# A four-layer latent-diffusion trunk in fp32: boundary and SiLU operations in place in PSUM, and the root of a row sum in six pointer steps

## The chip, the cores and the metric

The kernel runs on one core of a Trainium2 chip. The metric is the device time of one execution in microseconds (us); the kernel before took 2905.99 us, the median of three runs (2902.37 to 2906.01). The engines are TensorE (PE; PEld is its weight load), VectorE (DVE), ScalarE (ACT), GpSimd (POOL) and SyncE (SP, which issues the DMAs). Each works through its own queue in order; semaphores make one wait for another. SBUF is the working memory of 128 partitions; PSUM is the smaller memory into which PE writes, here eight banks of 128 x 512 fp32.

## What is computed

A trunk of four layers over 256 context tokens and 256 latent tokens of width 1024. Layers 0 and 3 mix tokens by differential attention, layer 1 by windowed grouped-query attention, layer 2 by a bidirectional Mamba-2 scan. Each mixer is followed by a SwiGLU feed-forward network (FFN). Every sub-layer is wrapped like this, with shift, scale and gate from a conditioning vector (adaLN); the last layer handles the latent tokens only:

```python
def rmsnorm(t, g):
    tf = tf * lax.rsqrt(jnp.mean(tf * tf, axis=-1, keepdims=True) + NORM_EPS)
...
    h_lat = h_lat + m_lat[:, 2] * rmsnorm(o_lat, norm_g[i, 1])
    u_lat = modulate(rmsnorm(h_lat, norm_g[i, 2]), m_lat[:, 3], m_lat[:, 4])
    h_lat = h_lat + m_lat[:, 5] * rmsnorm(swiglu(u_lat, ffn_w_in[i], ffn_w_out[i]), norm_g[i, 3])
```

So between any two blocks of matmuls each token row needs a root of the mean square of the sub-layer's output, a residual add, a root of the mean square of the sum, a scaling, and the adaLN modulation.

## The kernel before

**Tiling.** The 512 tokens are four tiles of 128: 0 and 1 are the context (stream `c`), 2 and 3 the latents (stream `l`). `hall` holds the residual stream h with tokens on the partitions, `uhall` and `ulall` the modulated input u with features on the partitions, split into a high part (rounded for the fast fp32 matmul) and the low remainder. Every product is three matmuls per 128-deep slice: high by high, low by high, high by low (`lin`, L285 to L287; `lin_tokens`, L295 to L297). Weights stream in by DMA; for each block ACT makes the high part (L261) and POOL subtracts it from the raw block, `wl = wr - wh`, 128 x 1024 (L263).

**A boundary.** The out-projection of a mixer, and of an FFN, ends in `project`: for each tile and half x of the 1024 features a PSUM bank `mm` is filled (L507); an FFN adds the partial sum in `o` (L511); `gated` takes the squares with their row sum on ACT (L429, junk output to tag `tm`) and multiplies by the gate row on DVE (L430). After the second half `residual` computes the root (L436 and `rsqrt`) and adds to h in one operation over 1024 features (L439). `after` then runs `prenorm`: squares of h (L447), root (L448 and `rsqrt`), scaling of one half by ACT (L456) and one by DVE (L454), eight transposes on PE into two `sm` banks (L460), modulation into a tile of tag `tm` alternately by ACT (L475) and DVE (L473), the high part by ACT (L477) and the low part by DVE (L478). The FFN's `unit` fills a bank `mm` and a bank `sc` (L555, L556), takes SiLU on ACT (L560), the product on DVE into the SBUF tile `hd` (L561), and splits it (L563, L564).

**Order and buffers.** A scheduler fixes the order on each engine before the program runs, from estimates of its own. The transposes of L460 thus stand at fixed places between the matmuls of other tiles. PSUM's eight banks are divided: `mm` three, `sc` two, `sm` two, `ad` one (which the scheduler also uses for other tiles at times). Tag `tm` has two buffers in SBUF. The adaLN vectors are finished by `ada_flush` (L346 is one of its DVE lines).

Of the kernel before, what the change touches and what calls it, by code (L numbers as in the profile page):

```python
# [22 lines left out]
NTT = NT // P  # L23
DEPTH = 4
# [153 lines left out]
class Trunk:  # L178
# [206 lines left out]

    def stat(self, groups, div):
# [38 lines left out]
    def gated(self, src, t, x, row, ss):  # L425

        nc = self.nc
        q = self.t([P, 512], "tm", 2)
        nc.scalar.activation(q, src, AF.Square, scale=1.0 / 32, accum_out=ss[:, x : x + 1])  # L429
        nc.vector.tensor_tensor(out=self.om[t][:, 512 * x : 512 * x + 512], in0=src, in1=row, op=AL.mult)  # L430

    def residual(self, t, ss):

        nc = self.nc
        y, m = (self.t([P, 1], f"rs_{x}1", 4) for x in ("y", "m"))
        nc.vector.tensor_scalar(out=m, in0=ss[:, 0:1], scalar1=ss[:, 1:2], scalar2=EPS, op0=AL.add, op1=AL.add)  # L436
        self.rsqrt(y, m, 1)
        h = self.hall[:, t, :]
        nc.vector.scalar_tensor_tensor(out=h, in0=self.om[t], scalar=y, in1=h, op0=AL.mult, op1=AL.add)  # L439

    def normed(self, t):

        nc = self.nc
        y, m, ss = (self.t([P, 1], f"rs_{x}1", 4) for x in ("y", "m", "s"))
        n = self.t([P, D], "sq", 2)
        h = self.hall[:, t, :]
        nc.scalar.activation(n, h, AF.Square, scale=1.0 / 32, accum_out=ss)  # L447
        nc.vector.tensor_scalar(out=m, in0=ss, scalar1=EPS, scalar2=None, op0=AL.add)  # L448
        self.rsqrt(y, m, 1)
        out = []  # L450
        for g in range(2):
            r = slice(512 * g, 512 * g + 512)
            if g:
                nc.vector.tensor_scalar(out=n[:, r], in0=h[:, r], scalar1=y, scalar2=None, op0=AL.mult)  # L454
            else:
                nc.scalar.activation(n[:, r], h[:, r], AF.Copy, scale=y)  # L456
            ps = self.psum("sm")
            for k in range(4):
                c = 512 * g + k * P
                nc.tensor.transpose(ps[:, k * P : (k + 1) * P], n[:, c : c + P], self.cst["ident"])  # L460
            out.append(ps.rearrange("p (k t) -> p k t", k=4))
        return out

    def modulate(self, src, shift, scale, t, g):
# [15 lines left out]
    def prenorm(self, shift, scale, t):  # L480
        for g, ps in enumerate(self.normed(t)):
            self.modulate(ps, shift, scale, t, g)
# [12 lines left out]
    def project(self, blocks, ah, al, streams, rows, after, add):  # L495
# [3 lines left out]
        for s in streams:  # L499
            ts = TILES[s]  # L500
            ss = {t: self.t([P, 2], "ss", 4) for t in ts}
            halves = [(t, x) for t in ts for x in range(2)]
            if s == streams[0]:
                halves = [(t, x) for x in range(2) for t in ts]
            for t, x in halves:
                ps = self.psum("mm")
                self.lin_tokens(ps, blocks[x], ah, al, t)  # L507
                src = ps
                if add:
                    src = self.om[t][:, 512 * x : 512 * x + 512]  # L510
                    nc.vector.tensor_tensor(out=src, in0=ps, in1=src, op=AL.add)  # L511
                self.gated(src, t, x, rows[s, x], ss[t])
                if x:
                    self.residual(t, ss[t])
                    after(t)
# [29 lines left out]
    def ffn(self, i, u, streams, pool, gate, after):  # L545
# [5 lines left out]
        def unit(j, wg, wu, s):  # L551
# [6 lines left out]
            hd = self.t([P, NT], "hd", 2, pool=pool)  # L558
# [879 lines left out]
```

## Time and profile before

| what | value |
|---|---|
| median of three runs | 2905.99 us |
| the profiled execution | 2899.41 us, span 2897.6 us |
| mean granted clock of TensorE | 0.961 |
| PE busy | 2620.8 us (90%) |
| DVE, ACT, POOL busy | 1574.4, 1236.4, 1098.3 us |
| POOL's weight subtractions, L263 | 356 of 2432 ns and 49 of 2426 ns |
| DMA | 355.40 MB, mean 123 GB/s |

A busy share says how much of the span an engine worked, not which engine held the others up: that is read from the list of waits, from the timeline of a stretch, and from the idle time that stands in brackets before an instruction, with the instruction that released it. The granted clock is the share of TensorE's full clock in a stretch.

### The profile page before, as it was taken

What the parts mean: (1) busy time and instruction counts of PE and PEld (TensorE: products, weight loads), DVE (VectorE), ACT (ScalarE), POOL (GpSimd) and SP (SyncE); (2) the same over time, 40 slices, a digit from 0 to 9 for tenths busy, and PEclk for the clock granted to TensorE, in tenths of its full rate; (3) what the DMA queues carried; (4) which work ended last, traced back from release to release, by engine and by line L of the source; (5) the groups of instructions that cost most, each with busy time, mean ns of one, the idle gap of its engine ahead of it and who ended that gap; (6) DMA issues with size and microseconds to landing.
All of it is one profiled execution on the core that took longest, in us unless ns stands there. A gap on an engine that the chain in (4) does not pass through costs nothing. (4 is left out here: it accounts for less than half of the span.)

```text
span 2897.6 us, 37494 instructions
## 1 busy us (share of the span) xinstructions
PE 2620.8 (90%) x14134; PEld 2110.0 (73%) x14134; DVE 1574.4 (54%) x2955; ACT 1236.4 (43%) x2439; POOL 1098.3 (38%) x525
## 2 busy tenths in 40 slices
PE   6999989999889989999888888879899998897898
PEld 3777677777776787777686666667777776786797
DVE  4676652222577662222588898866522226667444
ACT  4555443222357643222345555554432224554543
POOL 2322044334321053333333444433343343334585
PEclk8999999999999999999998999999999999999899
DMA  7433335544221145544231111132344442323352
GB/s 290 138 109 121 131 128 184 173 173 150 88 94 45 44 138 175 175 174 149 82 97 37 59 44 62 63 105 96 121 176 175 174 145 86 101 86 126 124 182 88
DMA packets 108325, 355.40 MB, mean 123 GB/s; under 512 B 14064, under 2 KB 24688, under 8 KB 105840
## 3 DMA queue, kind: packets, MB, share of 16 engines
q1 hardware_dynamic: 107568, 351.66, 36.0%
q8 instruction: 111, 1.82, 0.3%
q10 hardware_dynamic: 576, 1.34, 0.1%
q14 instruction: 70, 0.57, 0.1%
HBM read 329.36 MB, written 13.63 MB: 118 GB/s over the span
## 5 line engine op out<-in xcount | busy, mean ns | idle before, releaser
L263 POOL TENSOR_TENSOR wl<-wr,wh 128x1024 fp32r<-128x1024 f32 x356 | 863.5, 2432 | 1499.3 <-ACT wh L261 1360.0
L261 ACT ACTIVATE wh<-wr 128x1024 fp32r<-128x1024 f32 x356 | 376.0, 1057 | 809.4 <-PE mm L286 291.8
L285 PE MATMUL mm<-uh,wh 128*128 128x512 f32 (+1 forms) x1496 | 529.9, 355 | 16.3 <-ACT uh L477 15.0
L286 PE MATMUL mm<-ul,wh 128*128 128x512 f32 (+1 forms) x1496 | 526.9, 352 | 0.1
L287 PE MATMUL mm<-uh,wl 128*128 128x512 f32 (+1 forms) x1496 | 526.7, 352 | 0.0
L561 DVE TENSOR_TENSOR hd<-sc,sg 128x512 f32<-128x512 f32 (+1 forms) x100 | 56.9, 568 | 603.6 <-PE sc L287 599.0
L285 PEld LDWEIGHTS mm<-uh,wh 128*128 128x128 f32 x1496 | 289.3, 194 | 73.7 <-ACT uh L477 15.9
L287 PEld LDWEIGHTS mm<-uh,wl 128*128 128x128 f32 x1496 | 289.4, 193 | 34.4 <-issue 3.6
L286 PEld LDWEIGHTS mm<-ul,wh 128*128 128x128 f32 x1496 | 289.8, 194 | 32.5 <-issue 1.5
L285 PE MATMUL sc<-uh,wh 128*128 128x512 f32 (+1 forms) x800 | 273.7, 342 | 0.0
L287 PE MATMUL sc<-uh,wl 128*128 128x512 f32 (+1 forms) x800 | 273.7, 342 | 0.0
L286 PE MATMUL sc<-ul,wh 128*128 128x512 f32 (+1 forms) x800 | 273.6, 342 | 0.0
L296 PE MATMUL mm<-wh,hid 128*128 128x512 f32 x616 | 244.6, 397 | 0.0
L297 PE MATMUL mm<-wl,hid 128*128 128x512 f32 x616 | 244.0, 396 | 0.0
L295 PE MATMUL mm<-wh,hid 128*128 128x512 f32 x616 | 243.6, 396 | 0.0
L564 DVE TENSOR_TENSOR hid<-hd,hid 128x512 fp32r<-128x512 f32 (+1 forms) x100 | 207.5, 2075 | 65.8 <-ACT hid L563 65.8
L285 PEld LDWEIGHTS sc<-uh,wh 128*128 128x128 f32 x800 | 153.1, 191 | 17.6 <-issue 0.8
L286 PEld LDWEIGHTS sc<-ul,wh 128*128 128x128 f32 x800 | 153.2, 191 | 16.9
L287 PEld LDWEIGHTS sc<-uh,wl 128*128 128x128 f32 x800 | 153.2, 192 | 16.8
L595 DVE TENSOR_TENSOR o<-mm,o 128x512 f32<-128x512 f32 x84 | 58.0, 691 | 157.8 <-PE mm L297 157.8
L295 PEld LDWEIGHTS mm<-wh,hid 128*128 128x128 f32 x616 | 115.7, 188 | 35.9 <-ACT hid L563 4.2
L263 POOL TENSOR_TENSOR wl<-wa,wh 128x1024 fp32r<-128x1024 f32 x49 | 118.9, 2426 | 59.2 <-ACT wh L261 58.8
(300 smaller groups left out, 4851.5 us busy)
## 6 DMA issues: line engine op xcount, KB each, us to landing
wa<-in_adaw SPq DMA_DIRECT2D x192, 512.0 KB, 5.2
wr<-in_fin SPq DMA_DIRECT2D x154, 512.0 KB, 3.5
wr<-in_fout SPq DMA_DIRECT2D x77, 512.0 KB, 3.5
wr<-in_ssi SPq DMA_DIRECT2D x40, 512.0 KB, 3.5
wr<-in_daqk SPq DMA_DIRECT2D x24, 512.0 KB, 3.8
wa<-in_fin SPq DMA_DIRECT2D x22, 512.0 KB, 3.6
hspill<-h SPq DMA_DIRECT2D x8, 1024.0 KB, 4.0
h<-hspill SPq DMA_DIRECT2D x8, 1024.0 KB, 6.3
```

What stands on the lines that cost most here:

```text
L261: nc.scalar.activation(h, raw, AF.Copy)
L263: eng.tensor_tensor(out=l, in0=raw, in1=f32(h), op=AL.subtract)
L285: mm(out, wh, ah[ka][:, a:b], start=j == 0, stop=False)
L286: mm(out, wh, al[ka][:, a:b], start=False, stop=False)
L287: mm(out, wl, ah[ka][:, a:b], start=False, stop=j == len(todo) - 1)
L295: mm(out, ah[ka][:, tk], wt.h[:, kw, :], start=j == 0, stop=False)
L296: mm(out, al[ka][:, tk], wt.h[:, kw, :], start=False, stop=False)
L297: mm(out, ah[ka][:, tk], wt.l[:, kw, :], start=False, stop=j == len(todo) - 1)
L561: nc.vector.tensor_tensor(out=hd[:, :w], in0=pu[:, :w], in1=sg[:, :w], op=AL.mult)
L564: nc.vector.tensor_tensor(out=hl[:, a:b], in0=hd[:, :w], in1=f32(hh[:, a:b]), op=AL.subtract)
L595: nc.vector.tensor_tensor(out=o, in0=ps, in1=o, op=AL.add)
```

## The change

In `project` the second half goes to a bank `sc` instead of `mm`; the added partial sum, the gate product and the second half of the residual are written back into the bank they were read from. `residual` is two operations of 512 features, the first into `hall`, the second into PSUM, and a new ACT copy, `settle`, brings the latter to `hall` behind the transposes. The squares of h are taken in two halves. `modulate` writes back into the transposes' bank, and the FFN's product back into its `sc` bank. `rsqrt1` replaces `rsqrt` for one column: six operations of one form (TENSOR_SCALAR, whose scalars may be pointers to a value per partition) in place of nine of three forms; `rsqrt` stays for the rows of several columns in `stat`.

```diff
+G = 1024.0 / 27
...
+    def rsqrt1(self, m):
+        ts = self.nc.vector.tensor_scalar
+        y, b, a = (self.t([P, 1], f"rs_{x}1", 4) for x in "yba")
+        ts(out=b.bitcast(I32), in0=m.bitcast(I32), scalar1=-0.5, scalar2=1597463007.0 - 2.0**31, op0=AL.mult, op1=AL.add)
+        ts(out=a, in0=b, scalar1=b, scalar2=m, op0=AL.mult, op1=AL.mult)
+        ts(out=a, in0=a, scalar1=-10.0 / 3, scalar2=a, op0=AL.add, op1=AL.mult)
+        ts(out=b, in0=a, scalar1=5.0, scalar2=b, op0=AL.add, op1=AL.mult)
+        ts(out=a, in0=b, scalar1=b, scalar2=m, op0=AL.mult, op1=AL.mult)
+        ts(out=y, in0=a, scalar1=-64.0 / 3, scalar2=b, op0=AL.add, op1=AL.mult)
+        return y
...
-    def gated(self, src, t, x, row, ss):
...
+    def squares(self, src, ss):
         q = self.t([P, 512], "tm", 2)
-        nc.scalar.activation(q, src, AF.Square, scale=1.0 / 32, accum_out=ss[:, x : x + 1])
-        nc.vector.tensor_tensor(out=self.om[t][:, 512 * x : 512 * x + 512], in0=src, in1=row, op=AL.mult)
+        self.nc.scalar.activation(q, src, AF.Square, scale=G / 32, accum_out=ss)
...
+    def root(self, ss):
+        m = self.t([P, 1], "rs_m1", 4)
+        self.nc.vector.tensor_scalar(
+            out=m, in0=ss[:, 0:1], scalar1=ss[:, 1:2], scalar2=EPS * G * G, op0=AL.add, op1=AL.add
+        )
+        return self.rsqrt1(m)
...
+    def residual(self, t, ss, pss):
+        y = self.root(ss)
+        for x in range(2):
+            h = self.hall[:, t, 512 * x : 512 * x + 512]
+            self.nc.vector.scalar_tensor_tensor(
+                out=pss[1] if x else h, in0=pss[x], scalar=y, in1=h, op0=AL.mult, op1=AL.add
+            )
...
+    def settle(self, t, hp):
+        self.nc.scalar.activation(self.hall[:, t, 512:], hp, AF.Copy)
...
+    def normed(self, t, hp=None):
+        hs = [self.hall[:, t, :512], self.hall[:, t, 512:] if hp is None else hp]
+        ss = self.t([P, 2], "rs_s1", 4)
+        for x in range(2):
+            self.squares(hs[x], ss[:, x : x + 1])
+        y = self.root(ss)
...
+        if hp is not None:
+            self.settle(t, hp)
...
     def modulate(self, src, shift, scale, t, g):
-        tm = self.t([P, 4, P], "tm", 2)
...
             if k % 2:
-                nc.vector.tensor_scalar(out=tm[:, k], in0=src[:, k], scalar1=a, scalar2=b, op0=AL.mult, op1=AL.add)
+                nc.vector.tensor_scalar(out=src[:, k], in0=src[:, k], scalar1=a, scalar2=b, op0=AL.mult, op1=AL.add)
             else:
-                nc.scalar.activation(tm[:, k], src[:, k], AF.Identity, scale=a, bias=b)
+                nc.scalar.activation(src[:, k], src[:, k], AF.Identity, scale=a, bias=b)
...
-        nc.scalar.activation(uh, tm, AF.Copy)
-        nc.vector.tensor_tensor(out=ul, in0=tm, in1=f32(uh), op=AL.subtract)
+        nc.scalar.activation(uh, src, AF.Copy)
+        nc.vector.tensor_tensor(out=ul, in0=src, in1=f32(uh), op=AL.subtract)
...
             for t, x in halves:
-                ps = self.psum("mm")
+                ps = pss[t, x] = self.psum("sc" if x else "mm")
                 self.lin_tokens(ps, blocks[x], ah, al, t)
-                src = ps
                 if add:
-                    src = self.om[t][:, 512 * x : 512 * x + 512]
-                    nc.vector.tensor_tensor(out=src, in0=ps, in1=src, op=AL.add)
-                self.gated(src, t, x, rows[s, x], ss[t])
+                    o = self.om[t][:, 512 * x : 512 * x + 512]
+                    nc.vector.tensor_tensor(out=ps, in0=ps, in1=o, op=AL.add)
+                self.squares(ps, ss[t][:, x : x + 1])
+                nc.vector.tensor_tensor(out=ps, in0=ps, in1=rows[s, x], op=AL.mult)
                 if x:
-                    self.residual(t, ss[t])
-                    after(t)
+                    self.residual(t, ss[t], [pss[t, 0], ps])
+                    after(t, ps)
...
-                nc.vector.tensor_tensor(out=hd[:, :w], in0=pu[:, :w], in1=sg[:, :w], op=AL.mult)
+                nc.vector.tensor_tensor(out=pu[:, :w], in0=pu[:, :w], in1=sg[:, :w], op=AL.mult)
...
-            nc.scalar.activation(hh[:, a:b], hd[:, :w], AF.Copy)
-            nc.vector.tensor_tensor(out=hl[:, a:b], in0=hd[:, :w], in1=f32(hh[:, a:b]), op=AL.subtract)
+            nc.scalar.activation(hh[:, a:b], pu[:, :w], AF.Copy)
+            nc.vector.tensor_tensor(out=hl[:, a:b], in0=pu[:, :w], in1=f32(hh[:, a:b]), op=AL.subtract)
...
                         else:
+                            self.settle(t, hp)
                             self.nc.sync.dma_start(out=self.outs["out"][t - 2], in_=self.hall[:, t, :])
```

The order of each engine moves with it. The two places that follow are the ones the prediction speaks of; `rs_` tiles are the root's, `ss` the row sums, `ul_83` and `uh_82` the halves of u, `o_84` the SBUF tile `o`, and a number behind a name tells tiles apart.

DVE at the fourth boundary (FFN of layer 1 to the mixer of layer 2), after tile 2's second half is summed; the kernel before:

```order
L473 TENSOR_SCALAR tm_11946<-sm_11935,m_1697_9166,m_1696_9165 128x128
L473 TENSOR_SCALAR tm_11953<-sm_11941,m_1697_9166,m_1696_9165 128x128
L473 TENSOR_SCALAR tm_11946<-sm_11935,m_1697_9166,m_1696_9165 128x128
L511 TENSOR_TENSOR o_84<-mm_12078,o_84 128x512
L478 TENSOR_TENSOR ul_83<-tm_11946,uh_82 128x4x128
L473 TENSOR_SCALAR tm_11953<-sm_11941,m_1697_9166,m_1696_9165 128x128
L430 TENSOR_TENSOR o_84<-o_84,grow_11669 128x512
L478 TENSOR_TENSOR ul_83<-tm_11953,uh_82 128x4x128
L430 TENSOR_TENSOR o_84<-o_84,grow_11676 128x512
L436 TENSOR_SCALAR rs_m_2190_12021<-ss_11960 128x1
```

Here `sm_11935` and `sm_11941` are the transposed tile 1, and the two L430 are the gate products of tile 2. The kernel after, from the sum of tile 2's second half on:

```order
L534 TENSOR_TENSOR sc_11889<-sc_11889,o_84 128x512
L496 TENSOR_SCALAR sm_11834<-sm_11834,m_1671_9096,m_1670_9095 128x128
L536 TENSOR_TENSOR sc_11889<-sc_11889,grow_11580 128x512
L446 TENSOR_SCALAR rs_m_2137_11918<-ss_11858 128x1
L496 TENSOR_SCALAR sm_11834<-sm_11834,m_1671_9096,m_1670_9095 128x128
L496 TENSOR_SCALAR sm_11840<-sm_11840,m_1671_9096,m_1670_9095 128x128
L391 TENSOR_SCALAR rs_b_2139_11921<-rs_m_2137_11918 128x1
L392 TENSOR_SCALAR rs_a_2140_11922<-rs_b_2139_11921,rs_m_2137_11918 128x1
L393 TENSOR_SCALAR rs_a_2140_11922<-rs_a_2140_11922 128x1
L394 TENSOR_SCALAR rs_b_2139_11921<-rs_a_2140_11922,rs_b_2139_11921 128x1
L395 TENSOR_SCALAR rs_a_2140_11922<-rs_b_2139_11921,rs_m_2137_11918 128x1
L501 TENSOR_TENSOR ul_83<-sm_11834,uh_82 128x4x128
```

L534 is the add, L536 the gate product, L496 the modulation of tile 1 (`sm_11834`, `sm_11840`), L446 and L391 to L396 the root, L501 the low part. The gate product and the root of tile 2 stand between tile 1's modulations, where they stood behind them.

ACT between layer 3's mixer and its FFN, tiles 2 and 3; the kernel before:

```order
L447 ACTIVATE sq_22054,rs_s_4013_22053<-h_21885 128x1024
L261 ACTIVATE wh_22221<-wa_22220 128x1024
L456 ACTIVATE sq_22054<-h_21885,rs_y_4011_22051 128x512
L475 ACTIVATE tm_22080<-ad_22069,m_3122_16870,m_3123_16871 128x128
L475 ACTIVATE tm_22087<-sm_22075,m_3122_16870,m_3123_16871 128x128
L475 ACTIVATE tm_22080<-ad_22069,m_3122_16870,m_3123_16871 128x128
L475 ACTIVATE tm_22087<-sm_22075,m_3122_16870,m_3123_16871 128x128
L477 ACTIVATE uh_82<-tm_22080 128x4x128
L477 ACTIVATE uh_82<-tm_22087 128x4x128
L429 ACTIVATE tm_22119,ss_21951<-mm_22094 128x512
L447 ACTIVATE sq_22140,rs_s_4029_22139<-h_21885 128x1024
```

L429 is the Square of tile 3's second half (`mm_22094`); it stands behind all of tile 2's modulation. The kernel after:

```order
L441 ACTIVATE tm_21892,rs_s_3933_21891<-h_21727 128x512
L262 ACTIVATE wh_22051<-wr_22050 128x1024
L441 ACTIVATE tm_21894,rs_s_3933_21891<-sc_21850 128x512
L441 ACTIVATE tm_21958,ss_21793<-sc_21933 128x512
L262 ACTIVATE wh_22057<-wa_22056 128x1024
L479 ACTIVATE sq_21907<-h_21727,rs_y_3937_21898 128x512
L461 ACTIVATE h_21727<-sc_21850 128x512
L498 ACTIVATE ad_21909<-ad_21909,m_3070_16750,m_3071_16751 128x128
L441 ACTIVATE tm_21975,rs_s_3949_21974<-h_21727 128x512
L498 ACTIVATE sm_21915<-sm_21915,m_3070_16750,m_3071_16751 128x128
L441 ACTIVATE tm_21977,rs_s_3949_21974<-sc_21933 128x512
```

L441 is a Square, L479 the scaling, L461 `settle`, L498 the modulation. The Square of tile 3's second half (`sc_21933`) stands ahead of tile 2's scaling.

## Rows read from the trace of the kernel before

**Rows 1.** Page, part 1: engine, busy time, share of the span, instructions.

```profile
PE 2620.8 (90%) x14134; PEld 2110.0 (73%) x14134; DVE 1574.4 (54%) x2955; ACT 1236.4 (43%) x2439; POOL 1098.3 (38%) x525
```

**Rows 2.** Waits of PE: tile, line, releaser: us in total, times, longest us.

```profile
PE sm L460 <- ACT sq L456: 65.7, 21, 11.2
...
PE sm L460 <- DVE sq L454: 13.5, 3, 11.1
...
PE ad L460 <- DVE sq L454: 10.9, 1, 10.9
```

**Rows 3.** Windows of the boundaries (PE busy first, PEclk behind POOL); behind the fourth.

```profile
2671.00:2701.00 30.00, 7.58 (x36) 6.04 (x35) 20.84 (x50) 12.17 (x24) 7.36 (x4) 0.60 0.25 73
sum 158.00, PE 66.10 PEld 52.82 DVE 121.08 ACT 63.73 POOL 76.40; mean PE 9.44 PEld 7.55 DVE 17.30 ACT 9.10 POOL 10.91
...
1448.00:1455.00 7.00, 6.82 (x37) 6.82 (x38) 3.57 (x8) 4.61 (x12) 0.00 (x0) 0.59 0.18 70
```

**Rows 4.** Timeline, fourth boundary: start, duration, engine, line, [idle before, releaser].

```profile
1418.69 0.69 DVE L511 TENSOR_TENSOR o<-mm,o 128x512 f32<-128x512 f32 x1 [0.58 <-PE mm L297]
...
1435.68 0.15 DVE L376 TENSOR_SCALAR rs_y<-rs_m 128x1 int32<-128x1 int32 x1
...
1435.87 1.91 DVE L378 TENSOR_TENSOR rs_a<-rs_y 128x1 f32<-128x1 f32 x1
1437.82 2.26 DVE L379 TENSOR_TENSOR rs_a<-rs_a,rs_m 128x1 f32<-128x1 f32 x1
...
1444.73 2.19 DVE L382 TENSOR_TENSOR rs_a<-rs_y 128x1 f32<-128x1 f32 x1
...
1429.31 0.64 ACT L429 ACTIVATE tm<-o 128x512 f32<-128x512 f32 x1 [1.34 <-DVE ul L478]
...
1430.47 0.62 ACT L429 ACTIVATE tm<-o 128x512 f32<-128x512 f32 x1
...
1432.20 7.86 POOL L263 TENSOR_TENSOR wl<-wr,wh 128x1024 fp32r<-128x1024 f32 x3 [0.64 <-ACT wh L261]
...
1448.18 1.54 PE L460 MATMUL sm<-cst_base,sq 128*128 128x128 f32 x6 [11.22 <-ACT sq L456]
```

**Rows 5.** Single lines of DVE: min/median/max ns, first and last start, forms.

```profile
L379 DVE TENSOR_TENSOR rs_a<-rs_a,rs_m x74: 148/159/2342, 9.4 to 2891.4; 128x1 f32<-128x1 f32 x58, 128x4 f32<-128x4 f32 x16
...
L430 DVE TENSOR_TENSOR o<-o,grow x28: 680/692/2901, 742.5 to 2890.2; 128x512 f32<-128x512 f32 x28
L430 DVE TENSOR_TENSOR o<-mm,dq x12: 675/690/692, 337.1 to 2688.7; 128x512 f32<-128x512 f32 x12
...
L564 DVE TENSOR_TENSOR hid<-hd,hid x100: 415/2431/2451, 397.8 to 2867.6; 128x512 fp32r<-128x512 f32 x54, 128x256 fp32r<-128x256 f32 x46
...
L436 DVE TENSOR_SCALAR rs_m<-ss x28: 198/206/208, 336.8 to 2890.8; 128x1 f32<-128x1 f32 x28
...
L448 DVE TENSOR_SCALAR rs_m<-rs_s x30: 144/154/156, 8.8 to 2693.6; 128x1 f32<-128x1 f32 x30
...
L454 DVE TENSOR_SCALAR sq<-h,rs_y x30: 485/486/2645, 10.6 to 2695.3; 128x512 f32<-128x512 f32 x30
```

**Rows 6.** Timeline between layer 3's mixer and its FFN.

```profile
2687.98 0.60 ACT L429 ACTIVATE tm<-mm 128x512 f32<-128x512 f32 x1 [0.24 <-DVE ul L478]
...
2689.30 0.20 DVE L436 TENSOR_SCALAR rs_m<-ss 128x1 f32<-128x1 f32 x1
2689.54 0.15 DVE L376 TENSOR_SCALAR rs_y<-rs_m 128x1 int32<-128x1 int32 x1
...
2691.09 1.28 DVE L439 SCALAR_TENSOR_TENSOR h<-o,rs_y,h 128x1024 f32<-128x1024 f32 x1
...
2683.16 0.66 PE L460 MATMUL sm<-cst_base,sq 128*128 128x128 f32 x2 [11.07 <-DVE sq L454]
...
2695.96 0.45 PE L460 MATMUL ad<-cst_base,sq 128*128 128x128 f32 x1 [10.85 <-DVE sq L454]
...
2699.97 0.39 PE L285 MATMUL mm<-uh,wh 128*128 128x256 f32 x1
```

More of the change, by code (lines that the diff above doesn't have):

```diff
@@ L423, in gate_rows @@
         return rows
-    def gated(self, src, t, x, row, ss):
-        nc = self.nc
-        q = self.t([P, 512], "tm", 2)
-        nc.scalar.activation(q, src, AF.Square, scale=1.0 / 32, accum_out=ss[:, x : x + 1])
-        nc.vector.tensor_tensor(out=self.om[t][:, 512 * x : 512 * x + 512], in0=src, in1=row, op=AL.mult)
[L432 to L444, printed above, removed]
-        n = self.t([P, D], "sq", 2)
[L446 to L450, printed above, removed]
+    def squares(self, src, ss):
+        q = self.t([P, 512], "tm", 2)
+        self.nc.scalar.activation(q, src, AF.Square, scale=G / 32, accum_out=ss)
[15 more added lines that the diff above has]
+    def normed(self, t, hp=None):
+        nc = self.nc
+        hs = [self.hall[:, t, :512], self.hall[:, t, 512:] if hp is None else hp]
+        ss = self.t([P, 2], "rs_s1", 4)
+        for x in range(2):
+            self.squares(hs[x], ss[:, x : x + 1])
+        out = []
+        y = self.root(ss)
+        n = self.t([P, D], "sq", 2)
         for g in range(2):
@@ L453, in normed @@
             if g:
-                nc.vector.tensor_scalar(out=n[:, r], in0=h[:, r], scalar1=y, scalar2=None, op0=AL.mult)
+                nc.vector.tensor_scalar(out=n[:, r], in0=hs[g], scalar1=y, scalar2=None, op0=AL.mult)
             else:
-                nc.scalar.activation(n[:, r], h[:, r], AF.Copy, scale=y)
-            ps = self.psum("sm")
+                nc.scalar.activation(n[:, r], hs[g], AF.Copy, scale=y)
+            out.append(self.psum("sm"))
             for k in range(4):
                 c = 512 * g + k * P
-                nc.tensor.transpose(ps[:, k * P : (k + 1) * P], n[:, c : c + P], self.cst["ident"])
-            out.append(ps.rearrange("p (k t) -> p k t", k=4))
-        return out
+                nc.tensor.transpose(out[g][:, k * P : (k + 1) * P], n[:, c : c + P], self.cst["ident"])
+        if hp is not None:
+            self.settle(t, hp)
+        return [ps.rearrange("p (k t) -> p k t", k=4) for ps in out]
     def modulate(self, src, shift, scale, t, g):
@@ L472, in modulate, with prenorm @@
             if k % 2:
-                nc.vector.tensor_scalar(out=tm[:, k], in0=src[:, k], scalar1=a, scalar2=b, op0=AL.mult, op1=AL.add)
+                nc.vector.tensor_scalar(out=src[:, k], in0=src[:, k], scalar1=a, scalar2=b, op0=AL.mult, op1=AL.add)
             else:
-                nc.scalar.activation(tm[:, k], src[:, k], AF.Identity, scale=a, bias=b)
+                nc.scalar.activation(src[:, k], src[:, k], AF.Identity, scale=a, bias=b)
         uh, ul = (u[:, 4 * g : 4 * g + 4, t * P : (t + 1) * P] for u in (self.uhall, self.ulall))
-        nc.scalar.activation(uh, tm, AF.Copy)
-        nc.vector.tensor_tensor(out=ul, in0=tm, in1=f32(uh), op=AL.subtract)
-    def prenorm(self, shift, scale, t):
-        for g, ps in enumerate(self.normed(t)):
+        nc.scalar.activation(uh, src, AF.Copy)
+        nc.vector.tensor_tensor(out=ul, in0=src, in1=f32(uh), op=AL.subtract)
+    def prenorm(self, shift, scale, t, hp=None):
+        for g, ps in enumerate(self.normed(t, hp)):
             self.modulate(ps, shift, scale, t, g)
@@ L501, in project @@
             ss = {t: self.t([P, 2], "ss", 4) for t in ts}
+            pss = {}
             halves = [(t, x) for t in ts for x in range(2)]
@@ L1393, in run, with after @@
                 with self.tc.tile_pool(name=f"mix{i}", bufs=1) as pool:
-                    def after(t):
+                    def after(t, hp):
                         self.ada_flush(i, 4)
-                        self.prenorm(m[3], m[4], t)
+                        self.prenorm(m[3], m[4], t, hp)
                     for c in (("att",), ("att", "band"), ("ssd",))[i % 3]:
@@ L1406, in run, with after2 @@
                 with self.tc.tile_pool(name=f"ffn{i}", bufs=1) as pool:
-                    def after2(t):
+                    def after2(t, hp):
                         if nxt is not None:
                             self.ada_flush(nxt, 1)
-                            self.prenorm(self.m[nxt][0], self.m[nxt][1], t)
+                            self.prenorm(self.m[nxt][0], self.m[nxt][1], t, hp)
                         else:
+                            self.settle(t, hp)
                             self.nc.sync.dma_start(out=self.outs["out"][t - 2], in_=self.hall[:, t, :])
```

1 line of the change is left out of this document (removed).

## The prediction

> **What bounds the kernel now.** The page's first part comes first: TensorE (PE) is busy 2620.8 us of a span of 2897.6 [rows 1], so all that can be won, short of fewer matmuls, is its idle time and its slow clock. The second view lists what PE waits for, and the reader is to see that the largest entry is one line, L460, the four transposes that turn a normalised token tile before the next projection: 65.7 us behind ACT's scaling (L456), 13.5 and 10.9 us behind DVE's (L454) [rows 2]. They stand at fixed places in PE's in-order queue with the next tiles' matmuls behind them, so PE stands still when the chain that feeds them is late. No FFN line (L560 to L564) is in that list among the large entries. The third view cuts out the seven boundaries between a mixer and its FFN or an FFN and the next mixer. Seven stretches have 158.00 us with 66.10 us of PE work: 91.9 us idle, of which the last, from 2671 on, holds 30.00 − 7.58 = 22.4 and the first six 69.5. After a pause the granted clock stays near its lower level: in the 7 us behind the fourth boundary it is 0.59 [rows 3].
>
> Why is the chain late? The timeline of the fourth boundary (ffn of layer 1 to the mixer of layer 2) shows two reasons [rows 4]. First, tile 2's second half has its sum at 1418.69 + 0.69 = 1419.4, but the Squares that start its chain run on ACT only at 1429.31 and 1430.47, released by DVE's `ul` subtract (L478): the Square's junk output and the modulation of tile 1 share the two buffers of tag `tm`. That is 10 us lost before the chain begins. Second, DVE then runs steps of 0.15 us in 1.91 and 2.26 us while POOL subtracts weights (L263, three in 7.86 us from 1432.20). The 128x1 TENSOR_SCALAR of 0.15 us at 1435.68 goes through at its own speed under the same POOL work; the TENSOR_TENSOR of the same 128x1 behind it does not. PE's transposes start at 1448.18, 11.22 us late.
>
> Which forms suffer is read over all executions of a line [rows 5]. Two tensors from SBUF: L379 159 ns median and 2342 at most; L430 with both inputs in SBUF 692 and 2901; the FFN's L564 even 2431 at the median, against 415 for its shortest. One of two tensors from PSUM: L430 reading `mm` 690 median and 692 at most, so never stretched. TENSOR_SCALAR with 128x1, one pointer (L436) or none (L448): 208 and 156 ns at most in 58 executions. But the one-input L454, 128x512, went from 486 to 2645 ns: one input alone is no protection.
>
> **The change part by part.** *Boundary operations in PSUM.* The gate product, the added partial sum, the second half of the residual, the modulation and its `ul` subtract all get one operand in PSUM. None of them then has two SBUF tensors, the class that [rows 5] shows stretched. Their own length: the trace has no DVE or ACT instruction that writes PSUM. The nearest rows are the same forms from PSUM to SBUF, 690 ns for 128x512 [rows 5]; as a lower end I take nothing gained, as an upper end twice that, +0.69 us for each of some five operations in a chain, 3.4 us. I take the lower end, since reading PSUM in place of SBUF changed nothing (690 against 692 at the median).
>
> [...]
>
> *The `tm` buffers.* The modulation leaves them, so tile t+1's Square no longer waits for tile t's modulation. In DVE's order at the fourth boundary the new kernel has the gate product of tile 2 behind two pieces of tile 1's modulation, not behind all of it. The 10 us from 1419.4 to 1429.3 go.
>
> *The root.* Ten operations (with the sum of squares and epsilon) become seven TENSOR_SCALARs. Where one waits for the one before it, L436 starts 0.24 us ahead of the next [rows 6]; six steps at 0.24 and the sum are 1.65 us against 1.79 (2689.30 to 2691.09) undisturbed. So the shortening alone, two roots a tile, is worth 0.3 us; the freedom from POOL is worth much more: the chain of the fourth boundary lost 1.8 + 2.1 + 2.0 us in three steps [rows 4].
>
> *The added work.* The squares of h in two halves cost one more ACT instruction, but the first runs beside the second residual half. `settle`, an ACT copy of some 0.6 us (the L429 row of 0.60 at 2687.98 [rows 6]), comes after the scaling and delays no transposes; in the last layer it stands ahead of the output.
>
> *The sum at the six four-tile boundaries.* An undisturbed chain without the add is 7.98 us, 2687.98 to the transposes at 2695.96 [rows 6]. The new one: Square 0.7, product 0.6, root 1.65, two residual halves 1.2, the last square 0.75, root 1.65, scale 0.7, hand-over 0.5: about 7.8, with the add 8.5. The cover: in the kernel before, PE ran out of other work at 1448.18 − 11.22 = 1436.96, 17.5 us after tile 2's sum [rows 4]. The new order, counted in columns of the matmuls that stand between, puts the transposes about a quarter earlier; 10 to 13 us of cover are left from place to place, so 1.5 to 4 us of slack. I let 62 of the 69.5 us go; 7.5 stay for what still collides (L346 of the adaLN flush stands between the tiles with two SBUF inputs) and for the slots with only 9 us of cover.
>
> *Clock.* Behind the fourth boundary PE is busy 6.82 us at 0.59 [rows 3]; at full clock (1 − 0.59) × 6.82 = 2.8 us less. Seven such are 19.6; without the pauses I take 12, since other short stalls stay and pull the clock down too.
>
> *Layer 3's mixer to its FFN* has two tiles and nothing else on PE. In the kernel before, tile 3's Square starts at 2687.98, released by the end of tile 2's modulation, though the matmuls ended at 2683.16 − 11.07 = 2672.1; the FFN starts at 2699.97 [rows 6]. In the new order tile 3's squares and root are interleaved with tile 2's. From 2672.1: Square 0.7, product 0.6, the two tiles' roots sharing DVE some 3.3, residual 1.2, square 0.8, root 1.7, scale 0.7, then the 4.0 us that lie between 2695.96 and 2699.97: about 2685.5, with weight casts in between some 2687. Gain 13; 1 of it I give back for the low clock there: 12.
>
> *FFN.* `hd` in PSUM frees DVE of up to 2431 − 690 = 1741 ns in most of its 100 units [rows 5]; PE never waits there, so nothing. *Tail:* the copy adds 0.6 ahead of the output, the root gives 0.15 back: +0.5 us.
>
> Sum: −62 − 12 − 12 + 0.5 = −85.5. The profiled execution took 2899.4 us, 6.6 under the median 2906.0; on the median: 2820.5, I say 2821.
>
> **Rivals.** *A, the pointer steps collide too.* [...] As a mechanism here: three steps per chain still lose 2 us each, 6 us against some 3 of slack; 3 to 4.5 us stay at each of the seven boundaries, some 27, with 10 of the clock: 2821 + 37 = 2858. For it speaks L454, against it L436 and L448, and the step at 1435.68 that went through under POOL's work [rows 4].
>
> *B, writing PSUM is dear.* At twice 0.69 us some seven DVE operations of a tile, in the chain or queued before it, cost 4.8 us more, against 1.5 to 4 of slack: 2 to 2.5 us for each of 26 tiles, some 60 lost, 2881. No row of the kernel before speaks against it directly, since none writes PSUM from DVE; the equal reading does.
>
> *C, slower: PSUM banks held too long.* The second half sits in one of the two `sc` banks from its first matmul until `settle`, and `settle` stands in ACT's queue among weight casts (L261), which themselves wait for PE to free a buffer, up to the point where PE waits for the bank. `settle` is needed about 12 us after the tile's last matmul and should be done at 9.4. It decides from 85.5/28 = 3.1 us for each of 28 tiles; at 5 us of wait a tile it costs 140, 2821 + 140 = 2961. Against it: the order puts `settle` right behind the scaling, with no cast between.
>
> *D, the pauses are chain length, not collisions and buffers.* Then only 0.2 to 0.5 us a tile are won, 28 tiles, 6 to 14 us, and half of that where PE doesn't wait: 2901. Against it: the stretched steps stand in the trace with their POOL partners.
>
> **How the numbers follow.** Forecast 0.78, A 0.10, B 0.05, D 0.03, C 0.04. The forecast's own range: lower end with all 69.5, 19.6 of clock and 14 at layer 3, 2906 − 103 = 2803; upper end with 45, 8 and 10 of them, 2843. The range of 2803 to 2864 takes in A. A measurement of this kernel tells 0.2%, 6 us, from no change: faster 0.93 (forecast, A and B), within it 0.03 (D), slower 0.04 (C).
>
> **What would show it.** Right: in the changed profile the waits of PE for the transposes fall from 90 us to under 15; the root's six lines have maxima under 0.3 us; the Squares of a gate product start within 2 us of their sum; the clock in the 7 us behind a boundary is above 0.85; ffn 3 starts 13 us sooner after its mixer. Wrong, by A: root lines with maxima of 2 us; by B: the in-place lines at over 1 us without POOL beside them; by C: PE waits on `sc` with an ACT copy as releaser; by D: L460 still waits, with no stretched step in its chain.

## The result and the profile after

The kernel after takes 2830.44 us (median of 4 runs, 2825.74 to 2834.32) against 2904.65 us of the kernel before: a ratio of 0.9745, with a 95% interval of 0.9728 to 0.9761. That is 74 us, where 85 were forecast (2821, range 2803 to 2864). The profiled execution took 2834.32 us, 65.1 less than that of before. The page's first part, engine, busy time, share and instructions, answers to [rows 1]:

```profile
PE 2623.4 (93%) x14134; PEld 2098.7 (74%) x14134; DVE 1348.9 (48%) x2809; ACT 1242.3 (44%) x2527; POOL 1090.4 (38%) x525
```

PE's busy time has not fallen (2620.8 to 2623.4). So the profiled 65 us are idle time of PE alone (276.8 us before, 209.1 after), though the mean granted clock is better (0.974 for 0.961): something has eaten what the clock gave. DVE's 1574.4 us have become 1348.9.

The waits of PE after (engine, tile, line, releaser, us in total, times, longest) answer to [rows 2]; L483 is the transposes, L479 ACT's scaling:

```profile
PE sm L483 <- ACT sq L479: 26.0, 11, 5.4
...
PE mm L286 <- ACT uh L500: 10.2, 2, 8.3
...
PE ad L483 <- ACT sq L479: 3.9, 1, 3.9
```

From 90 us in 25 waits the transposes' waits have come down to 29.9 in 12, the longest from 11.2 to 5.4. The middle line is a wait of the first projections; before it was 15.0 us, with one of 12.9. The windows of the same seven boundaries, and the 7 us behind the fourth (PE busy first, granted clock behind POOL's busy time), answer to [rows 3]:

```profile
2604.00:2634.00 30.00, 20.01 (x89) 15.98 (x87) 19.53 (x59) 20.57 (x43) 11.77 (x5) 0.77 0.37 121
sum 163.00, PE 130.80 PEld 110.91 DVE 104.79 ACT 114.79 POOL 95.55; mean PE 18.69 PEld 15.84 DVE 14.97 ACT 16.40 POOL 13.65
...
1419.00:1426.00 7.00, 6.97 (x60) 6.98 (x60) 3.43 (x9) 4.63 (x12) 0.00 (x0) 1.00 0.36 150
```

The idle time of the seven is now 163.00 − 130.80 = 32.2 us (91.9 before): 10.0 at the last one (22.4) and 22.2 at the six others (69.5). That is 59.7 us; the other 8 us of idle time went outside these stretches, 4.6 of them in that first wait. Behind the fourth boundary the clock is 1.00 where it was 0.59. Behind the last boundary it went the other way: in the 7 us behind it the clock is 0.78 (from 2634), where the kernel before has 1.00 (from 2701).

Single lines of DVE (minimum, median and maximum in ns) answer to [rows 5]: a step with two pointers, the steps with one, the gate product in place, the residual's PSUM half, the scaling out of PSUM, and the FFN's subtract.

```profile
L395 DVE TENSOR_SCALAR rs_a<-rs_b,rs_m x58: 258/273/276, 10.4 to 2826.2; 128x1 f32<-128x1 f32 x58
...
L393 DVE TENSOR_SCALAR rs_a<-rs_a x58: 202/214/215, 9.9 to 2825.7; 128x1 f32<-128x1 f32 x58
...
L536 DVE TENSOR_TENSOR sc<-sc,grow x14: 699/700/700, 742.3 to 2824.4; 128x512 f32<-128x512 f32 x14
...
L456 DVE SCALAR_TENSOR_TENSOR sc<-sc,rs_y,h x27: 742/750/752, 338.9 to 2827.4; 128x512 f32<-128x512 f32 x27
...
L477 DVE TENSOR_SCALAR sq<-sc,rs_y x25: 740/751/753, 342.2 to 2627.5; 128x512 f32<-128x512 f32 x25
...
L587 DVE TENSOR_TENSOR hid<-sc,hid x100: 414/678/693, 378.8 to 2801.7; 128x512 fp32r<-128x512 f32 x54, 128x256 fp32r<-128x256 f32 x46
```

None of these is ever stretched: the largest maximum is 753 ns. Writing into PSUM costs what reading it cost (700 against 690 ns), so the upper end of the prediction's bound for it (twice 0.69 us) is off by far; but the steps with pointers take 214 to 273 ns, and not the 150 of a step without. The same modulation and low part run at the start of the kernel on an SBUF tile (`o`), and there they are stretched as before; the last line is the low part with its PSUM operand:

```profile
L496 DVE TENSOR_SCALAR o<-o,m,m x8: 338/341/2516, 39.2 to 41.0; 128x128 f32<-128x128 f32 x8
...
L501 DVE TENSOR_TENSOR ul<-o,uh x4: 676/679/2451, 43.5 to 46.4; 128x512 fp32r<-128x512 f32 x4
...
L501 DVE TENSOR_TENSOR ul<-sm,uh x54: 675/682/693, 58.8 to 2632.3; 128x512 fp32r<-128x512 f32 x54
```

So two pointers do not protect a step of 128x128 from SBUF (2516 ns); the root's steps, never over 276, have one column.

### The profile page after: what moved, and what is told of

It is laid out like the page before. It is cut to its first block, busy times and chain, and to the rows that moved or that the text cites. A ratio compares the mean times of both kernels' runs of the same rounds, so it can differ in the third digit from the quotient of the medians.

```text
span 2832.5 us, 37450 instructions
## 1 busy us (share of the span) xinstructions
PE 2623.4 (93%) x14134; PEld 2098.7 (74%) x14134; DVE 1348.9 (48%) x2809; ACT 1242.3 (44%) x2527; POOL 1090.4 (38%) x525
## 5 line engine op out<-in xcount | busy, mean ns | idle before, releaser
L584 DVE TENSOR_TENSOR sc<-sc,sg 128x512 f32<-128x512 f32 (+1 forms) x100 | 57.7, 577 | 757.8 <-PE sc L288 748.8
L296 PE MATMUL mm<-wh,hid 128*128 128x512 f32 x504 | 201.4, 400 | 0.0
L298 PE MATMUL mm<-wl,hid 128*128 128x512 f32 x504 | 199.5, 396 | 0.0
L297 PE MATMUL mm<-wh,hid 128*128 128x512 f32 x504 | 198.8, 394 | 0.0
L320 PE MATMUL ad<-wa,act 128*32 128x512 f32 x768 | 113.3, 611 | 14.7 <-DMA wa<-in_adaw 14.7
L1183 POOL TENSOR_TENSOR cd<-h,dtt 128x512 f32<-128x512 f32 x64 | 78.7, 1234 | 123.9 <-DVE dm L1193 118.6
```

The lines of the kernel that those rows point to most:

```text
L296: mm(out, ah[ka][:, tk], wt.h[:, kw, :], start=j == 0, stop=False)
L297: mm(out, al[ka][:, tk], wt.h[:, kw, :], start=False, stop=False)
L298: mm(out, ah[ka][:, tk], wt.l[:, kw, :], start=False, stop=j == len(todo) - 1)
L320: nc.tensor.matmul(self.adaps[g : g + 32, :], self.act[:, k, :], w[:, b, :], start=k == 0, stop=k == KD - 1, skip_group_check=True, tile_p ...
L584: nc.vector.tensor_tensor(out=pu[:, :w], in0=pu[:, :w], in1=sg[:, :w], op=AL.mult)
L1183: getattr(nc, self.ENG_CD).tensor_tensor(out=cd.rearrange("p (c l) -> p c l", c=4), in0=cbm[d].rearrange("p (c l) -> p c l", c=4), in1=sel ...
```

## The experiments

A kernel whose name begins with b_ is the kernel before with one thing changed, one with a_ is the kernel after with one or more. Each ratio is to the kernel before on the same chip; its median there lay between 2901.29 and 2904.65 us, so a difference between two medians of this table can be off by some 3 us.

| kernel | median us | ratio to before, interval |
|---|---|---|
| after | 2830.44 | 0.9745 [0.9728, 0.9761] |
| b_root: six-step root alone | 2878.88 | 0.9909 [0.9883, 0.9935] |
| b_mod: modulation in place alone | 2877.06 | 0.9910 [0.9893, 0.9926] |
| b_junk: a buffer for the junk alone | 2896.62 | 0.9979 [0.9969, 0.9988] |
| a_oldroot: after, root of nine steps | 2885.40 | 0.9935 [0.9915, 0.9954] |
| a_modsb: after, modulation in SBUF | 2867.04 | 0.9877 [0.9863, 0.9892] |
| a_ffnsb: after, FFN product in SBUF | 2833.20 | 0.9758 [0.9742, 0.9775] |
| b_nopool | 2693.31 | 0.9280 [0.9267, 0.9294] |
| a_nopool | 2677.68 | 0.9223 [0.9210, 0.9237] |
| b_shift: before, weights 128 bytes on | 2910.22 | 1.0026 [1.0015, 1.0037] |
| a_shift: after, weights 128 bytes on | 2824.02 | 0.9728 [0.9712, 0.9743] |
| a_sp4: a_shift, POOL in quarters | 2774.27 | 0.9557 [0.9539, 0.9575] |
| a_slp4: a_sp4, lambda's own buffers | 2768.51 | 0.9540 [0.9521, 0.9558] |

**The root alone** (`rsqrt1` of the diff in place of `rsqrt(y, m, 1)`).

> The kernel before with the six-step pointer root alone; everything else, the shared tm buffers too, as before. If POOL's collisions in the root steps are what makes the chains late (52 of about 89 us of stretched time at the boundaries lie in them), some 40 to 50 us of the change's 74 come back: 2855 to 2865. If the late start behind the shared buffers is the whole cause, 0 to 5 us: 2900. If each of the two takes what cover there is, about 25: 2880. In all cases the root's lines show maxima under 0.3 us; if pointer steps collide, maxima near 2 us and no gain.

Measured: 24 us, the size of the joint theory; yet the waits of PE in its profile fell by far more:

```profile
PE sm L475 <- ACT sq L471: 27.2, 15, 7.0
...
PE ad L475 <- DVE sq L469: 10.9, 1, 10.9
...
PE sm L475 <- DVE sq L469: 9.2, 5, 5.2
```

Its transposes' waits are 47.3 us against 90.1, and all idle time of PE is 2876.0 − 2638.6 = 237 against 277. Its busy time, however, is 2638.6 us, 18 more than before: the root brings a cost with it that has nothing to do with DVE. The runs on the weights' place take that up: beside b_shift, whose weights lie where those of b_root do, the root alone is worth 31 us.

**A buffer for the Squares' junk.**

```diff
-        q = self.t([P, 512], "tm", 2)
+        q = self.t([P, 512], "tj", 1, mybir.dt.bfloat16)
```

> The kernel before with one edit: the Squares' junk output goes to a buffer of its own (one, bf16), so that it no longer shares the two tm buffers with the modulation. All collisions stay. If the shared buffers are the cause, 50 to 60 us come back: 2850. If collisions alone are, 0: 2905. If both count, about 30: 2875. The Square of tile 2's second half at the fourth boundary should start within 2 us of its sum (before: 11 us).

Measured: 6 us. Two lines more of the kernel before, start of the root and of the residual of tile 2 at the fourth boundary (start, duration):

```profile
1435.45 0.20 DVE L436 TENSOR_SCALAR rs_m<-ss 128x1 f32<-128x1 f32 x1
...
1441.08 1.28 DVE L439 SCALAR_TENSOR_TENSOR h<-o,rs_y,h 128x1024 f32<-128x1024 f32 x1
```

The same boundary in b_junk, from the sum of tile 2's second half on (PE's row ends with the idle time before it), tells why it is so little:

```profile
1423.65 0.69 DVE L511 TENSOR_TENSOR o<-mm,o 128x512 f32<-128x512 f32 x1 [0.22 <-PE mm L297]
...
1426.83 0.20 DVE L436 TENSOR_SCALAR rs_m<-ss 128x1 f32<-128x1 f32 x1
...
1428.93 2.15 DVE L378 TENSOR_TENSOR rs_a<-rs_y 128x1 f32<-128x1 f32 x1
1431.11 2.33 DVE L379 TENSOR_TENSOR rs_a<-rs_a,rs_m 128x1 f32<-128x1 f32 x1
1433.47 2.32 DVE L380 SCALAR_TENSOR_TENSOR rs_a<-rs_a 128x1 f32<-128x1 f32 x1
...
1437.08 1.28 DVE L439 SCALAR_TENSOR_TENSOR h<-o,rs_y,h 128x1024 f32<-128x1024 f32 x1
...
1446.91 1.97 PE L460 MATMUL sm<-cst_base,sq 128*128 128x128 f32 x8 [10.42 <-ACT sq L456]
```

PE comes to this tile 5 us later here, so times are counted from the tile's sum, 1424.3 (1419.4 in [rows 4]). The Square follows it by 0.5 us, as expected, and the root (L436) by 2.5, where it was 16.1. But the root now runs under POOL from its first steps: three of them lose 6.3 us (two lost 3.9 before), and the residual (L439) starts 12.7 us after the sum (21.7 before). The edit also moved the order: PE runs out of other work 12.2 us after the sum, where it was 17.6, so it still waits 10.42 us in place of 11.22. Over the whole kernel its waits for the transposes are 97.7 us, more than the 90.1 before. The late start was real, and its end by itself was worth little.

**The modulation in place, alone** (`tm = src` in `modulate`).

> The kernel before with the modulation alone in place in PSUM: tm is freed and the ul subtract and the modulation lose their collisions; root, gate product, residual and FFN as before. It should gain what the junk buffer alone gains and a little more (15 us of stretched time lie in the ul subtract): 2850 if the buffers are the cause, 2895 if the root's collisions are, 2865 if both.

Measured: 26 us, between the cases. The Squares no longer share `tm` with the modulation, as in b_junk; the other 20 of the 26 are the modulation's and the subtract's own collisions, the buffers that tiles' modulations shared among themselves, or the moved order. The runs don't part these.

**POOL without reading.**

```diff
-        eng.tensor_tensor(out=l, in0=raw, in1=f32(h), op=AL.subtract)
+        if eng is nc.gpsimd:
+            eng.memset(f32(l), 0.0)
+        else:
+            eng.tensor_tensor(out=l, in0=raw, in1=f32(h), op=AL.subtract)
```

> The kernel before, in which POOL writes zeros into the low parts of the weights and does not subtract (this leaves out the low part of every weight that POOL splits; the time is what counts). POOL then reads nothing from SBUF beside DVE. If the collisions are the cause, 60 to 75 us come back although the buffers stay shared: 2830 to 2845. If the shared buffers are, 10 to 20: 2890. If both, about 45: 2860. The maxima of L378 to L383 should fall from 2.3 us to under 0.3; if they stay, POOL's reads are not what stretches DVE.

> The kernel after, in which POOL writes zeros into the low parts of the weights and does not subtract (this leaves out the low part of every weight that POOL splits). If the change has freed the boundaries of POOL, what it gives is what the collisions in the mixers cost: 0 to 10 us, 2820 to 2830. If a good part of the 30 us that PE still waits at the boundaries is collisions, 20 us or more: under 2812.

Measured: 209 us less than before, and 153 less than the kernel after; both theories were far too small. A line of the root with two SBUF tensors, in the kernel before with POOL quiet:

```profile
L382 DVE TENSOR_TENSOR rs_a<-rs_a,rs_m x74: 149/160/165, 9.7 to 2688.4; 128x1 f32<-128x1 f32 x58, 128x4 f32<-128x4 f32 x16
```

Its maximum is 165 ns; with POOL's subtractions the same line (L379 in [rows 5]) reaches 2342. So POOL's subtractions are what stretches these steps; the fill writes SBUF as they do, but reads nothing. POOL still runs a few products that read SBUF (`cd` of the Mamba-2 scan, 78 us): all 16 stretched executions of DVE's `dm<-dm,cd` in b_nopool (up to 1777 ns, median 692) lie beside one of these, and none beside a fill alone. Without the subtractions the two kernels are 15.6 us apart, not 74: some four fifths of what the change gives is escape from collisions (nearly three quarters, if the 6 to 8 us of the weights' place, below, are added to both differences). The other 150 us were a miss of mine: I had counted collisions at the boundaries only, and the mixers have them too (PE's wait for `dm` in the scan is 38.5 us in the kernel after, 21.1 in a_nopool). The 150 is not the collisions' price alone: the order of all engines has moved in these two kernels, and the fill is shorter, 955 against 2432 ns.

**Parts taken out of the kernel after.** For a_oldroot `root` calls `rsqrt(y, m, 1)` again; for a_modsb `modulate` writes to `self.t([P, 4, P], "tm", 2)`; for a_ffnsb the product goes to `hd`.

> The kernel after with the old root of nine steps of two tensors; all the rest as after. If the collisions of the root are the main cause, 40 to 50 us are lost: 2875. If the shared buffers were, 0 to 5: 2833. If both, the earlier start leaves cover for most of it, and 10 to 20 are lost: 2845.

> The kernel after with the modulation in the two tm buffers in SBUF again, shared with the Squares; root, gate product, residual and FFN in place as after. If the shared buffers are the main cause, 40 to 60 us are lost: 2880. If the root's collisions were, 5 to 10 (the ul subtract collides again): 2838. If both, about 25: 2855.

> The kernel after with the FFN's product in the SBUF tile hd again: its 100 subtracts collide with POOL again. PE never waited for them, so within 5 us of the kernel after: 2826 to 2835. A rival has it that DVE's freed 170 us count at the end of each FFN, where the boundary's chain queues behind them: 15 us or more lost, 2845.

The old root costs 55 us in the kernel after, three quarters of the gain, though in the kernel before the new one gave 24. It also puts the weights back in their old place (next part); beside a_shift, which has them there too, it costs 61. Waits of PE in a_oldroot:

```profile
PE sm L485 <- ACT sq L481: 65.4, 14, 10.0
...
PE ad L485 <- ACT sq L481: 11.8, 1, 11.8
```

77 us again, although every other part is in place: the cover does not hold against root steps that reach 2.4 us and more (2411 ns at most for its L379, 4749 for its L381). The modulation in SBUF costs 37 us; whether by the shared buffers or by its collisions is not parted by this sum. The FFN's product is worth 2.8 us, inside the two intervals: the 147 us of DVE that it frees (1496.3 against 1348.9) were off the path, as forecast.

At one boundary the two causes can be told apart, the one between layer 3's mixer and its FFN, where PE has nothing else to do. Its waits there, in us, from each run's timeline:

| kernel | for tile 2's transposes | for tile 3's |
|---|---|---|
| before | 11.07 | 10.85 |
| b_junk: no shared junk buffer | 11.65 | 5.54 |
| b_root: six-step root (L393, L394 at most 216 ns) | 5.23 | 10.87 |
| b_nopool: no subtractions | 2.96 | 10.86 |
| a_oldroot | 11.80 | 6.05 |
| a_modsb | 3.34 | 10.69 |
| after | 3.85 | 5.45 |

The first wait follows the root's collisions. The second does not: it stays at 10.9 without any subtraction of POOL, and falls to 5.5 where Squares and modulation do not share `tm`. So of the 12 us won there some 5 are the buffers'.

**The place of the weights.** The kernels so far with the new root have more busy time on PE than the same kernels with the old one (b_root 2638.6 us against 2620.8, a_nopool 2585.6 against b_nopool's 2576.7, after 2623.4 against a_oldroot's 2617.2). Their root tags take 128 bytes more of SBUF ahead of the weights. One edit moves the weights and leaves the order of every engine as it was:

```diff
-        ss = self.t([P, 2], "rs_s1", 4)
+        ss = self.t([P, 2], "rs_s1", 8)
```

> The kernel before, its order of instructions unchanged on every engine, with four more 32-byte buffers of a tag that is allocated ahead of the weights: all weight tiles lie 128 bytes further on, where they lie in every kernel with the new root. If the place of the weights is what makes the 512-column matmuls of lin start every 231 to 232 ns in place of 227, some 3800 of them cost 4.5 ns more: 17 us slower, 2920, with the spacing near 231. If the new root's instructions are the cause in some other way, nothing changes: 2903 and 227 ns.

> The kernel after, its order unchanged on every engine, with the same four buffers more: the weights move on by 128 bytes, to the place modulo 256 that they had in the kernel before. If the place is the cause, 17 us faster than the kernel after, 2813, and a spacing of 227 ns. If not, 2830 and 231 ns.

Matmuls of one FFN block with 512 columns (start, duration), the first and the eighth of a run in the kernel before:

```profile
502.97 0.39 PE L285 MATMUL sc<-uh,wh 128*128 128x512 f32 x1
...
504.55 0.39 PE L286 MATMUL sc<-ul,wh 128*128 128x512 f32 x1
```

And the first and the eighth of such a run in b_shift:

```profile
491.23 0.40 PE L285 MATMUL sc<-uh,wh 128*128 128x512 f32 x1
...
492.87 0.39 PE L286 MATMUL sc<-ul,wh 128*128 128x512 f32 x1
```

Seven starts in 1.58 us are 226 ns each, seven in 1.64 us are 234; in both, u is the moving operand and the weights the stationary one. Over the some 3500 such pairs that each trace has at a granted clock of 1, the median is 227 ns in the kernel before and in a_shift, and 232 in b_shift and in the kernel after, as expected. PE's busy time rises from 2620.8 to 2635.3 us in b_shift, and falls from 2623.4 to 2617.1 in a_shift. In time it is less than I expected, +7.7 us (interval 1.0015 to 1.0037) and −6.4 (−4.3 if each is set against the kernel before on its chip; the intervals of a_shift and the kernel after overlap): the granted clock moves against it, 0.964 in b_shift for 0.961 and 0.968 in a_shift for 0.974. So the shift is shown by the spacing, both ways, and by b_shift's interval, which lies clear of 1; a_shift's own gain is likely, not settled.

**Shorter POOL instructions.** If a DVE step waits for the POOL instruction that runs, shorter ones make it wait less:

```diff
+        flat = [x.rearrange("p k n -> p (k n)") for x in (l, raw, f32(h))]
+        step = kc * w // (4 if eng is nc.gpsimd else 1)
+        for c in range(0, kc * w, step):
+            o, x, y = (f[:, c : c + step] for f in flat)
+            eng.tensor_tensor(out=o, in0=x, in1=y, op=AL.subtract)
```

> As a_shift, and each of POOL's weight subtractions is cut into four instructions of a quarter (256 columns). If a DVE step with two SBUF tensors waits for the end of the POOL instruction that runs, no such step waits longer than a quarter, some 0.6 us in place of 2.4: the maxima of the mixers' two-tensor steps fall from over 2 to under 1 us, and a good part of the 150 us that went when POOL read nothing comes back, 60 to 110: 2705 to 2755. If waiting is shared out per byte and not per instruction, the stretched steps stay as long, and so does the kernel: 2813, or some us more for POOL's extra instructions.

Measured: 50 us less than a_shift, somewhat under the lower end forecast. DVE and ACT have the same order in both, so it is the shorter instructions and not the order. One step of the SSD mixer with two SBUF tensors (min/median/max ns) in the kernel before:

```profile
L1132 DVE TENSOR_TENSOR v<-h,wst x48: 405/410/2593, 1539.0 to 1915.1; 128x256 f32<-128x256 f32 x48
```

The same step in a_sp4:

```profile
L1159 DVE TENSOR_TENSOR v<-h,wst x48: 407/412/1372, 1471.8 to 1829.0; 128x256 f32<-128x256 f32 x48
```

And POOL's subtractions in a_sp4, grouped (busy us, mean ns):

```profile
L268 POOL TENSOR_TENSOR wl<-wr,wh 128x256 fp32r<-128x256 f32 x1420 | 1049.8, 775 | 1221.8 <-ACT wh L262 1048.6 <-PE ad L324 52.3 <-PE mm L301 36.2
```

The maximum falls from 2593 to 1372 ns, not to a quarter. A piece takes 775 ns in the mean, more than a quarter of 2432; and a step can also sit through more than one piece when they follow each other, as a 128x1 step of differential attention (its `sm` is an SBUF tile) does at 104.71 beside four pieces of POOL (start, duration):

```profile
104.71 2.23 DVE L824 TENSOR_TENSOR sm<-sm,neglam 128x1 f32<-128x1 f32 x1
...
104.12 2.80 POOL L268 TENSOR_TENSOR wl<-wr,wh 128x256 fp32r<-128x256 f32 x4
```

**Lambda's own buffers** (tags `lamp` and `lamq` in place of `tm` for the two tiles of `da_lambda`).

> As a_sp4 (weights 128 bytes further on, POOL's subtractions in quarters), and layer 3's lambda vectors get buffers of their own in place of the two tm buffers, so that their DMA is issued long before and no longer stands between the last two steps of a root in DVE's queue. At the boundary to layer 3's mixer PE waits 7.84 us in a_sp4, 7.68 of them while DVE waits for that DMA: 6 to 9 us faster than a_sp4 with the clock, 2766. If the wait only passes to the next thing that is late there, less than 3: 2772.

It came from the profile after, at the boundary to layer 3's mixer (DVE, then PE):

```profile
2402.74 0.27 DVE L395 TENSOR_SCALAR rs_a<-rs_b,rs_m 128x1 f32<-128x1 f32 x1
2408.07 0.29 DVE L785 TENSOR_TENSOR tm<-tm 128x128 f32<-128x128 f32 x1 [5.05 <-DMA tm<-in_lam]
2408.28 0.21 DVE L396 TENSOR_SCALAR rs_y<-rs_a,rs_b 128x1 f32<-128x1 f32 x1
...
2409.29 1.12 PE L483 MATMUL sm<-cst_base,sq 128*128 128x128 f32 x4 [5.26 <-ACT sq L479]
```

Between the last two root steps there (L395, L396) DVE waits 5.05 us for a DMA into a `tm` buffer, since L785 stands between them in its queue. a_slp4 is 5.8 us under a_sp4 (4.6 if each is set against the kernel before on its chip). The two intervals overlap and the order of DVE and ACT moved as well, so the gain is not settled; that PE no longer waits a microsecond at that boundary is seen in its timeline. It is the fastest version: 0.954 of the kernel before.

## Why the prediction was right, and where it missed

- *The number.* The mechanism held, but that 2830 lies so near 2821 is in part luck: the pauses and PE's busy time each gave some 15 us less than forecast, while 8 came from outside the boundaries and 9 lie between the profiled executions and the medians (65.1 us against 74).
- *The boundaries' pauses end.* Right in kind, smaller in size: at the six four-tile boundaries 47.3 us of 69.5 went, and 62 had been forecast. One 5.3 us piece of the rest is the lambda DMA, which no term had.
- *The signs.* The transposes' waits were to fall under 15 us: they are 29.9. The clock behind a boundary was to be above 0.85: it is 1.00 behind six and 0.78 behind the last. The Squares follow their sum within 2 us in 34 of 36 cases, the other two after 3.5 and 4.0 (at the fourth boundary tile 2's follows by 0.9). The root's lines stay under 0.3 us, and the last FFN starts 12.3 us sooner after its mixer (15.5 for 27.9; 13 forecast).
- *The chain is about 7.8 us.* Too short. Between layer 3's mixer and its FFN, tile 2's chain after is, on ACT, DVE, ACT, DVE and PE (start, duration):

```profile
2611.56 0.60 ACT L441 ACTIVATE tm<-sc 128x512 f32<-128x512 f32 x1 [0.23 <-PE sc L298]
...
2616.15 1.04 ACT L262 ACTIVATE wh<-wr 128x1024 fp32r<-128x1024 f32 x1
2617.10 0.58 ACT L441 ACTIVATE tm<-sc 128x512 f32<-128x512 f32 x1
...
2612.89 0.20 DVE L446 TENSOR_SCALAR rs_m<-ss 128x1 f32<-128x1 f32 x1
...
2614.69 0.75 DVE L456 SCALAR_TENSOR_TENSOR h<-mm,rs_y,h 128x512 f32<-128x512 f32 x1
...
2617.80 0.21 DVE L446 TENSOR_SCALAR rs_m<-rs_s 128x1 f32<-128x1 f32 x1 [1.69 <-ACT tm L441]
...
2620.90 1.12 PE L483 MATMUL ad<-cst_base,sq 128*128 128x128 f32 x4 [3.85 <-ACT sq L479]
```

From 2611.56 to 2620.90 it takes 9.3 us. The root (2612.89 to 2614.69) is 1.80 us, no shorter than the old one undisturbed, because two-pointer steps take 273 ns; a weight cast of 1.04 us stands between the two Squares, and tile 3's first steps stand among those of the second root (2617.80 to 2620.1). The six steps are worth nothing by their number: what they buy is that none of them was stretched beside POOL (276 ns at most in the kernel after, where the old root's L379 reached 2342).
- *Layer 3's mixer to its FFN:* 12.4 us of idle time gone (22.4 to 10.0), 12 forecast. The terms of that boundary's sum add up to 2685.1 and not 2685.5, which changes nothing.
- *Clock and busy time.* I forecast 12 us from the clock. Behind the fourth boundary it came (1.00 for 0.59), but PE's busy time rose all the same, by 2.6 us: the weights' new place took back 14.5 us of busy time by b_shift, 6.3 by a_shift. No term had it, and the order of instructions cannot show it. Without it PE's busy time would be 4 to 12 us lower than before; how much of the 12 is the clock's is not settled. That other short stalls pull the clock down too was my estimate, and the windows after do not settle it: at the fourth boundary PE is idle 3.9 of 18 us at a clock of 1.00, at the one to layer 3's mixer 8.4 of 30 at 0.83.
- *Buffers or collisions.* The prediction gave both as reasons for the lateness. The buffers alone are worth 6 us (b_junk), the collisions most of it (a_oldroot, the two kernels without POOL's subtractions). At layer 3's boundary the buffers held tile 3 by themselves.
- *In-place operations cost the same:* right for two tensors, 700 ns. The prediction says that the kernel before has no DVE instruction that writes PSUM; it has one, layer 1's band mask, added in place to the scores (busy us, mean ns):

```profile
L900 DVE TENSOR_TENSOR sc<-sc,cst_band 128x128 f32<-128x128 f32 x21 | 6.0, 290 | 1.1 <-PE sc L671 1.0
```

It takes 300 ns at most over its 32 executions, so rival B could have been weighed before. For the scaling the same cost is not right. L477, one tensor, takes 486 ns at the median from SBUF (the four tiles at the start) and 751 from PSUM; it stands beside ACT's scaling of some 720 ns and adds nothing to the chain. Why PSUM costs more there no run shows.
- *Rivals.* A falls: no root step is stretched in the kernel after (maximum 276 ns). B falls by the 700 ns. C falls: no wait of PE is put down to `settle` (L461). D falls with b_nopool and, for tile 3 at layer 3's boundary, with b_junk.

## What to carry to other kernels

Where GpSimd works on SBUF beside a chain of small VectorE steps, look at the maximum of each line, not its mean: a step with two SBUF tensors can cost a whole GpSimd instruction (0.16 us became 2.3 here, beside subtractions of 2.4). A PSUM operand in place of one of them freed it (the gate product reached 2.9 us before and 0.70 after); so did a pointer scalar in place of the second tensor, but only for steps of one column (0.28 us at most): a TENSOR_SCALAR of 128x128 or 128x512 from SBUF still reached 2.5 and 2.6 us. An earlier start did little for a chain that then met the same obstacle (b_junk: a wait of 10.42 us at the fourth boundary for 11.22). After an edit of small tiles, compare the busy time of untouched lines: the place of the large tiles may have moved (128 bytes were 14.5 us of PE's busy time in b_shift).

## What the runs showed that I had not expected

- The same 512-column matmuls, same order, start every 227 or 232 ns (medians of a trace) as the weights lie 128 bytes apart; in b_shift that is 14.5 us of PE's busy time. Why the place matters is open.
- Cutting POOL's subtraction into quarters raises its work from 985 us (356 of 2432 ns and 49 of 2426 before) to 1192 (1049.8 + 142.6), and the kernel is 50 us faster.
- Up to some 150 us of the kernel after still go to POOL's subtractions beside DVE (a_nopool, in which the order has moved too).
